# Gated linear attention layer: all values and gates ahead of the heads, parked in DRAM, instead of head by head

## The chip, the cores and the metric

The kernel runs on one core of one Trainium2 chip. The metric is the device time of one execution in microseconds (us). Three executions of the kernel before took 945.23, 946.44 and 946.85 us, median 946.44 us.

TensorE (PE in the profile) does the matrix products, with its weight loads shown apart as PEld. VectorE is DVE, ScalarE is ACT, GpSimd is POOL, and SyncE (SP) only issues DMAs here. Each engine works through its own queue of instructions strictly in the order written for it.

## The reference, cut to what matters

Two layers run on a sequence of 512 rows of 1024 channels. The first (a state-space branch and a convolution branch) is not touched by the change. The second is gated linear attention with four heads:

```python
u = rms_norm(x, norm_pre[i])
p = u @ od_w_in[j]                       # 1024 -> 2*1024 + 2*2048 + 16
q, k, v, r, lr = split(p)                # queries, keys, values, gates, low rank
g = log_sigmoid(lr @ w_gate_up + b_gate) / 16
# per head: q, k 256 wide, v 512 wide; b = running sum of g inside a chunk of 64 rows
# S_t = diag(exp(g_t)) S_{t-1} + k_t^T v_t ;  o_t = q_t S_t     (causal)
o = rms_norm(o, norm_g) * silu(r)        # per head
x = x + rms_norm(concat(o) @ od_w_out[j], norm_post[i])
```

Values and gates of a head depend only on `u` and weights. The decays `b` enter queries and keys only.

## The kernel before

**Precision and tiles.** Every product is made from operands split into a high and a low part, so one 128x128 weight tile times 512 columns costs three matmuls (high*high, high*low, low*high). Weights come in blocks of 512 KB (128 x 1024 fp32) from the list `wlist` (lines 85 to 110), in the order of use. `w_raw` (line 113) issues the load of a block on SP into one of three `wraw` buffers. `w_split` (line 134) makes the high part with a cast on ACT (line 143, two `wh` buffers) and, in this layer, the low part with a subtraction on DVE (line 149, three `wl` buffers). One block feeds 24 matmuls. `w_get` (line 167) hands out a block and has the next one split ahead.

**The second layer's stages, per head.**
- `values(h)` (line 960) and `gate(h)` (line 965): both call `proj_mv` (line 804), four weight blocks and 96 matmuls (lines 800 to 802) into four PSUM banks of the tag `mm`, one for each 128 rows. `values` splits each bank into `vh` and `vl` (line 963; `split` at line 191 is a cast on ACT, line 193, and a subtraction on DVE, line 194). `gate` puts SiLU on it (ACT, line 970) and multiplies by the norm's gain on POOL (line 971). There is one `vh` and one `vl` for all heads. Gates lie in buffers of the tag `sb`, eight in all.
- queries and keys (lines 1010 to 1064): four weight blocks, 96 matmuls by `mm_st` (line 181) with one `mm` bank a block, and then for each bank a chain on DVE, ACT and POOL that multiplies by the exponentials of the running sums of decays `bcum` and splits the result (`qr` into `qh`, `ql`; `kr` into `kh`, `kl`). `sums(h)` (line 988) is the running sum, two scans on DVE.
- scores (lines 1070 to 1093): 42 small matmuls (line 1078) into `aux` banks, three of them, masked into `at` on DVE (line 1083) and split into `ah`, `al`.
- outputs (lines 1105 to 1130): 30 matmuls (lines 1113 to 1115), in four parts of 128 rows; each part goes through a square sum on ACT, a reciprocal root of seven small DVE steps (lines 200 to 209), a product with the gate on DVE (line 1125), four transposes on PE (line 1128, one `cv` bank) and a split into `oth`, `otl`.
- the output projection: its first half (heads 0 and 1) is done at head 2 (lines 1097 to 1103) and kept in DRAM as `yp_d`; the second half comes in `proj_tail` (line 872) after head 3, whose first part again is a `proj_mv` of 96 matmuls, block by block over the channels, head 2's first.

In program order the layer is: values(0); decays (lines 976 to 996); gate(0); then for each head queries and keys, values (but for head 0), the next head's sums, scores, gate (but for head 0), at head 2 the first half of the output projection, and outputs.

**What sets the real order.** The program is planned when it is built (`TileContext(..., schedule_with_timeline_sim=True)`, line 1213): a planner plays the engines through with estimated durations, and gives each engine the ready instruction that comes first in program order. `feed()` (line 156) moves an instruction 1500 places ahead; the weight splits and `split` use it. So work that is ready fills gaps left by work that comes before it in the program. What the planner wrote is then fixed for each queue, and an instruction that is late on the chip holds all behind it on its engine.

**Temporaries.** `tmp()` (line 74) gives one of five buffers of the tag `t2`; a buffer comes free when its last reader, a DMA included, is done.

Of the kernel before, what the change touches and what calls it, by code (L numbers as in the profile page):

```python
# [9 lines left out]
F32 = mybir.dt.float32  # L10
F32R = mybir.dt.float32r
I32 = mybir.dt.int32
AF = mybir.ActivationFunctionType
ALU = mybir.AluOpType
# [3 lines left out]
P = 128  # L18
D = 1024
S = 512  # L20
KT = D // P
TT = S // P
# [9 lines left out]
HEADS = 4  # L32
# [19 lines left out]
def trunk(ctx: ExitStack, tc: tile.TileContext, A: dict, out: bass.AP, dbg: dict | None = None):  # L52
    nc = tc.nc
    V, G, SC, PE, SY = nc.vector, nc.gpsimd, nc.scalar, nc.tensor, nc.sync
# [7 lines left out]
    dram = ctx.enter_context(tc.tile_pool(name="dram", bufs=1, space=DRAM))  # L62
# [7 lines left out]
    def ps(tag="mm"):  # L70
        n = banks["bufs"][tag]
        return banks["pool"].tile([P, S], F32, tag=tag, bufs=n, name=f"ps_{tag}")

    def tmp(shape=(P, S), dt=F32, name="tmp"):
        return t2.tile(list(shape), dt, tag="t2", name=name)
# [9 lines left out]
    wlist = []  # L85
# [14 lines left out]
    for n in range(2):  # L100
        for j in range(4):
            wlist.append(A["w_out0"][n, 4 + j])
    for h in range(HEADS):
        wv, wr = ([A["w_vr"][o + h, j] for j in range(4)] for o in (0, 4))
        wqk = [A["w_qk"][2 * h + j] for j in range(2)] + [A["w_qk"][8 + 2 * h + j] for j in range(2)]
        wlist.extend(wv + wr + wqk if h == 0 else wqk + wv + wr)
        if h >= 2:
            for n in range(2):
                for j in range(4):
                    wlist.append(A["w_out1"][n, (h - 2) * 4 + j])  # L110
    wst = {"next_raw": 0, "next_split": 0, "raw": {}, "hl": {}, "low": {}}

    def w_raw():
# [42 lines left out]
    def feed():  # L156
        return tc.high_priority(offset=1500)
# [9 lines left out]
    def w_get():  # L167
        i = wcur[0]
        wcur[0] += 1
        while wst["next_split"] <= min(i + 1, len(wlist) - 1) and wst["next_split"] not in w_resident:  # L170
            w_split()
        return wst["hl"].pop(i)
# [8 lines left out]
    def mm_st(acc, w, xh, xl):  # L181
        wh, wl = w
        whv = wh.rearrange("p (k c) -> p k c", c=P)
        wlv = wl.rearrange("p (k c) -> p k c", c=P)
        for k in range(KT):
            PE.matmul(acc, whv[:, k, :], xh[:, k, :], start=(k == 0), stop=False)  # L186
            PE.matmul(acc, whv[:, k, :], xl[:, k, :], start=False, stop=False)  # L187
        for k in range(KT):
            PE.matmul(acc, wlv[:, k, :], xh[:, k, :], start=False, stop=(k == KT - 1))  # L189

    def split(h, l, src, eng=V):
        with feed():
            SC.copy(h, src)
            eng.tensor_tensor(out=l, in0=src, in1=h.bitcast(F32), op=ALU.subtract)  # L194
# [56 lines left out]
    def bigt(dt, name):  # L251
        return big.tile([P, KT, S], dt, tag="big", name=name)
# [475 lines left out]
    def sbt_(shape, dt, name):  # L728
        return sbp.tile(list(shape), dt, tag="sb", name=name)
# [30 lines left out]
    csum, vs, rstd, rt, v = ln[:, 0, :], (ln[:, 1, :], ln[:, 2, :]), ln[:, 3, :], ln[:, 4, :], ln[:, 0, :]  # L760
# [31 lines left out]
    def mm_mv(accs, w, xh, xl, k0, kt0, first, last):  # L792

        wh, wl = w
        for j in range(2):
            kt = kt0 + j
            whj, wlj = wh[:, j * S:(j + 1) * S], wl[:, j * S:(j + 1) * S]
            for tt in range(TT):
                ts_ = slice(tt * P, (tt + 1) * P)
                PE.matmul(accs[tt], xh[:, kt, ts_], whj, start=(first and j == 0), stop=False)  # L800
                PE.matmul(accs[tt], xl[:, kt, ts_], whj, start=False, stop=False)  # L801
                PE.matmul(accs[tt], xh[:, kt, ts_], wlj, start=False, stop=(last and j == 1))  # L802

    def proj_mv(xh, xl, blocks=()):
        accs = [ps("mm" if i < banks["bufs"]["mm"] else "aux") for i in range(TT)]
        for j in range(4):
            mm_mv(accs, blocks[j] if blocks else w_get(), xh, xl, 0, 2 * j, j == 0, j == 3)
        return accs

    yp = rp.tile([P, TT, D], F32, tag="r16", name="yp")  # L810
    for n in range(2):
        accs = proj_mv(yfh, yfl)
# [56 lines left out]
    u1h = bigt(F32R, "u1h")  # L869
    u1l = bigt(F32R, "u1l")  # L870
# [61 lines left out]
    L1 = ExitStack()  # L932
    LQ = ExitStack()
    pa = L1.enter_context(tc.tile_pool(name="l1a", bufs=1, side="right", reuse_waits="tile"))
    vh = pa.tile([P, TT, S], F32R, name="vh")
    vl = pa.tile([P, TT, S], F32R, name="vl")
    bcum = pa.tile([P, KT, S], F32, name="bcum")
    ng = pa.tile([P, S], F32, name="ng")
# [21 lines left out]
    def values(blocks=()):  # L960
        accs = proj_mv(u1h, u1l, blocks)
        for tt in range(TT):
            split(vh[:, tt, :], vl[:, tt, :], accs[tt])

    def gate(h):
        accs = proj_mv(u1h, u1l)
        rg = []
        for tt in range(TT):
            r_ = sbt_((P, S), F32, f"rg{h}{tt}")
            SC.activation(r_, accs[tt], AF.Silu)  # L970
            G.tensor_tensor(out=r_, in0=r_, in1=ng, op=ALU.mult)  # L971
            rg.append(r_)
        return rg

    values(vblocks)
    az = pg.tile([P, KT, S], F32, name="az")
    for kt in range(KT):
# [10 lines left out]
    def sums(h):  # L988

        for kt in (2 * h, 2 * h + 1):  # L990
            V.tensor_tensor_scan(out=bcum[:, kt, :], data0=reset, data1=bcum[:, kt, :], initial=0.0, op0=ALU.mult, op1=ALU.add)  # L991

    for kt in range(KT):
        V.tensor_sub(bcum[:, kt, :], bcum[:, kt, :], az[:, kt, :])
        if kt == 1:
            sums(0)
    rg = gate(0)
    PG.close()

    pb = L1.enter_context(tc.tile_pool(name="l1b", bufs=1, side="right", reuse_waits="tile"))  # L1000
    pq = LQ.enter_context(tc.tile_pool(name="l1q", bufs=1, side="right", reuse_waits="tile"))
    R_OFF = (0, 448, 768, 960)
    NQ = 1152
# [1 line left out]
    COL = {(0, 0): None, (0, 3): 0, (0, 2): 128, (0, 1): 256, (1, 3): 384, (1, 2): 512, (2, 3): 640}  # L1005

    yp_d = dram.tile([S, D], F32, name="yp_d")
    for h in range(HEADS):

        qh = pq.tile([P, 2, NQ], F32R, tag="qh", name=f"qh{h}")  # L1010
        ql = pq.tile([P, 2, NQ], F32R, tag="ql", name=f"ql{h}")
        kh = pq.tile([P, 2, 896], F32R, tag="kh", name=f"kh{h}")
        kl = pq.tile([P, 2, 896], F32R, tag="kl", name=f"kl{h}")
        eb, en, el = [], [], []
        for j in range(2):
            kt = 2 * h + j
# [10 lines left out]
        for j in range(2):  # L1027
# [8 lines left out]
            for i in range(4):  # L1036
                o = R_OFF[i]

                dst = qr[:, o:o + 256].rearrange("p (a t) -> p a t", t=128)[:, :, 0:64] if o + 256 <= NQ else None
                src = acc[:, i * P:(i + 1) * P].rearrange("p (a t) -> p a t", t=64)  # L1040
# [12 lines left out]
        for j in range(2):  # L1053
            acc = ps()
            mm_st(acc, w_get(), u1h, u1l)
            kr = pq.tile([P, 896], F32, tag="raw", bufs=1, name=f"kr{h}{j}")
            ec, es = el[j]
            V.tensor_mul(kr[:, 0:S], acc, en[j])
            fac = small.tile([P, 3, 2], F32, tag="fac", bufs=2, name=f"fac{h}{j}")
            V.tensor_copy(fac[:, :, 0], es[:, 0:3])  # L1060
            V.tensor_copy(fac[:, :, 1], ec.rearrange("p (i a) -> p i a", a=2)[:, 0:3, 1])
            G.tensor_tensor(out=kr[:, S:896].rearrange("p (i t) -> p i t", t=64), in0=kr[:, 0:384].rearrange("p (i t) -> p i t", t=64),  # L1062
                            in1=fac.rearrange("p i a -> p (i a)").unsqueeze(2).to_broadcast([P, 6, 64]), op=ALU.mult)
            split(kh[:, j, :], kl[:, j, :], kr)
        if h:
            values()
        if h + 1 < HEADS:
            sums(h + 1)

        ah = pb.tile([P, 1280], F32R, tag="ah", name=f"ah{h}")  # L1070
        al = pb.tile([P, 1280], F32R, tag="al", name=f"al{h}")
# [8 lines left out]
        for jj in range(4):  # L1080
# [5 lines left out]
            if jj < 3:  # L1086
                q0, n = OFFD[jj]
# [3 lines left out]
                w_ = (384, 256, 128)[jj]  # L1091
                split(ah[:, c0:c0 + w_], al[:, c0:c0 + w_], acc[:, 0:w_])
        split(ah[:, 0:S], al[:, 0:S], at.rearrange("p j t -> p (j t)"))
        if h:
            rg = gate(h)

        if h == 2:
            for n in range(2):
                accs = proj_mv(*oa)
# [3 lines left out]
                    SY.dma_start(yp_d[tt * P:(tt + 1) * P, n * S:(n + 1) * S], yt)  # L1103

        if h % 2 == 0:
            oth = pb.tile([P, KT, S], F32R, tag="oth", bufs=1, name=f"oth{h}")
            otl = bigt(F32R, f"otl{h}")
        acol = {(0, 3): 512, (0, 2): 640, (0, 1): 768, (1, 3): 896, (1, 2): 1024, (2, 3): 1152}
        for i in range(4):
# [20 lines left out]
            split(oth[:, k0:k0 + 4, i * P:(i + 1) * P], otl[:, k0:k0 + 4, i * P:(i + 1) * P], tp.rearrange("p (k t) -> p k t", t=P))  # L1130
        if h == 1:
            oa = (oth, otl)
    LQ.close()

    E1 = ExitStack()
# [9 lines left out]
    proj_tail(oth, otl, yp, bigt, x1_d, gpost1, tail1)  # L1145
    E1.close()
    L1.close()
    SBP.close()
    L0.close()

# [66 lines left out]
```

## Time and profile before

| | us |
|---|---|
| median of three executions | 946.44 |
| the profiled execution's own time | 946.38 |
| its span, first to last instruction | 944.7 |
| PE busy | 897.7 (95% of the span) |
| weight loads of PE busy | 718.9 (76%) |
| DVE busy | 641.9 (68%) |
| ACT busy | 485.1 (51%) |
| POOL busy | 245.4 (26%) |
| PE's mean granted clock | 0.981 |

Busy time is the time in which an engine works on at least one instruction. Matmuls overlap: each shows some 0.39 us from start to end, but the next starts 0.23 us later. The granted clock is the share of full speed that PE is given. A line of the timeline reads: start, duration, engine, line of the kernel, operation, result, operands, count, and in brackets the idle time before it with what ended it. The second layer's first matmuls begin shortly after 500 us.

### The profile page before, as it was taken

What the parts mean: (1) busy time and instruction counts of PE and PEld (TensorE: products, weight loads), DVE (VectorE), ACT (ScalarE), POOL (GpSimd) and SP (SyncE); (2) the same over time, 40 slices, a digit from 0 to 9 for tenths busy, and PEclk for the clock granted to TensorE, in tenths of its full rate; (3) what the DMA queues carried; (4) which work ended last, traced back from release to release, by engine and by line L of the source; (5) the groups of instructions that cost most, each with busy time, mean ns of one, the idle gap of its engine ahead of it and who ended that gap; (6) DMA issues with size and microseconds to landing.
All of it is one profiled execution on the core that took longest, in us unless ns stands there. A gap on an engine that the chain in (4) does not pass through costs nothing. (4 is left out here: it accounts for less than half of the span.)

```text
span 944.7 us, 12134 instructions
## 1 busy us (share of the span) xinstructions
PE 897.7 (95%) x4396; PEld 718.9 (76%) x4396; DVE 641.9 (68%) x1206; ACT 485.1 (51%) x693; POOL 245.4 (26%) x258
## 2 busy tenths in 40 slices
PE   5995998999999999999999979999999999999996
PEld 4873776777778877778887758888888888888875
DVE  7953999999989989832579477584483232744546
ACT  6542786786678855564444566343543242523430
POOL 2693657463123422011054002000200020000222
PEclk8998999999999999999999979999999999999998
DMA  9877987787988885288463112212212223324412
GB/s 278 228 198 194 229 199 184 178 205 204 215 220 228 210 231 179 92 224 201 153 215 124 45 63 93 84 37 82 90 67 90 73 83 135 134 89 164 193 45 89
DMA packets 54955, 142.74 MB, mean 151 GB/s; under 512 B 14256, under 2 KB 15792, under 8 KB 54896
## 3 DMA queue, kind: packets, MB, share of 16 engines
q1 hardware_dynamic: 46832, 112.62, 35.9%
q0 software_dynamic: 8064, 29.36, 17.3%
q8 instruction: 34, 0.56, 0.2%
q14 instruction: 25, 0.20, 0.1%
HBM read 95.18 MB, written 13.22 MB: 115 GB/s over the span
## 5 line engine op out<-in xcount | busy, mean ns | idle before, releaser
L143 ACT CAST wh<-wraw 128x1024 fp32r<-128x1024 f32 x126 | 132.1, 1048 | 161.4 <-PE ps_mm L801 92.5
L149 DVE TENSOR_TENSOR wl<-wraw,wh 128x1024 fp32r<-128x1024 f32 x70 | 87.0, 1243 | 115.2 <-ACT wh L143 114.8
L655 DVE SCALAR_TENSOR_TENSOR ps_cv<-h,cw,ps_cv 128x512 f32<-128x512 f32 x232 | 161.7, 745 | 2.7 <-ACT ps_cv L652 1.8
L186 PE MATMUL ps_mm<-u0h,wh 128*128 128x512 f32 x320 | 129.9, 407 | 1.0 <-ACT tmp L679 0.7
L187 PE MATMUL ps_mm<-u0l,wh 128*128 128x512 f32 x320 | 129.4, 405 | 0.0
L800 PE MATMUL ps_mm<-wh,u1h 128*128 128x512 f32 x240 | 96.2, 402 | 3.5 <-ACT wh L143 3.4
L801 PE MATMUL ps_mm<-wh,u1l 128*128 128x512 f32 x240 | 96.3, 401 | 0.8 <-DVE u1l L194 0.8
L131 POOL DMA_DIRECT2D wl<-wraw x56 | 48.9, 884 | 182.4 <-ACT wl L130 178.2
L802 PE MATMUL ps_mm<-wl,u1h 128*128 128x512 f32 x240 | 91.6, 401 | 1.6 <-DVE wl L149 1.6
L189 PE MATMUL ps_mm<-u0h,wl 128*128 128x512 f32 x320 | 82.5, 395 | 1.1 <-DMA wl<-wraw 1.1
L186 PEld LDWEIGHTS ps_mm<-u0h,wh 128*128 128x128 f32 x320 | 61.8, 193 | 16.4 <-issue 1.6
L130 ACT ACTIVATE wl<-wraw 128x1024 fp32r<-128x1024 f32 x56 | 59.2, 1057 | 25.8 <-DMA wraw<-in_w_in_dram 14.0
L187 PEld LDWEIGHTS ps_mm<-u0l,wh 128*128 128x128 f32 x320 | 61.7, 193 | 13.9 <-issue 1.1
L189 PEld LDWEIGHTS ps_mm<-u0h,wl 128*128 128x128 f32 x320 | 59.4, 188 | 14.9 <-DMA wl<-wraw 1.5
L800 PEld LDWEIGHTS ps_mm<-wh,u1h 128*128 128x128 f32 x240 | 45.9, 191 | 14.9 <-ACT wh L143 3.8
L971 POOL TENSOR_TENSOR rg<-rg,ng 128x512 f32<-128x512 f32 x16 | 24.2, 1544 | 124.6 <-ACT rg L970 124.6
L802 PEld LDWEIGHTS ps_mm<-wl,u1h 128*128 128x128 f32 x240 | 45.6, 191 | 13.1 <-DVE wl L149 2.3
L801 PEld LDWEIGHTS ps_mm<-wh,u1l 128*128 128x128 f32 x240 | 45.9, 191 | 11.7 <-DVE u1l L194 1.2
L186 PE MATMUL ps_mm<-u1h,wh 128*128 128x512 f32 x128 | 50.7, 396 | 0.0
L187 PE MATMUL ps_mm<-u1l,wh 128*128 128x512 f32 x128 | 50.5, 394 | 0.0
L1062 POOL TENSOR_TENSOR kr<-kr,fac 128x384 f32<-128x384 f32 x8 | 6.7, 837 | 124.2 <-DVE rr L205 65.1
L800 PE MATMUL ps_mm<-wh,oth 128*128 128x512 f32 x96 | 37.8, 396 | 0.5 <-ACT wh L143 0.5
(341 smaller groups left out, 1993.6 us busy)
## 6 DMA issues: line engine op xcount, KB each, us to landing
wl<-wraw POOLq DMA_DIRECT2D x56, 512.0 KB, 6.1
wraw<-in_w_in_dram SPq DMA_DIRECT2D x40, 512.0 KB, 5.2
wraw<-in_w_out_dram SPq DMA_DIRECT2D x32, 512.0 KB, 3.3
wraw<-in_w_vr_dram SPq DMA_DIRECT2D x32, 512.0 KB, 3.2
wraw<-in_w_qk_dram SPq DMA_DIRECT2D x16, 512.0 KB, 3.3
tm<-kt_d SPq DMA_DIRECT2D x8, 512.0 KB, 6.3
wraw<-in_w_glu_dram SPq DMA_DIRECT2D x8, 512.0 KB, 5.8
wraw<-in_w_pw_dram SPq DMA_DIRECT2D x8, 512.0 KB, 5.1
```

The source lines that it names most:

```text
L130: SC.activation(l, raw, AF.Copy, scale=-1.0)
L131: G.dma_start(l.bitcast(F32), raw, accum_op=ALU.add)
L143: SC.copy(h, raw)
L149: V.tensor_tensor(out=l, in0=raw, in1=h.bitcast(F32), op=ALU.subtract)
L186: PE.matmul(acc, whv[:, k, :], xh[:, k, :], start=(k == 0), stop=False)
L187: PE.matmul(acc, whv[:, k, :], xl[:, k, :], start=False, stop=False)
L189: PE.matmul(acc, wlv[:, k, :], xh[:, k, :], start=False, stop=(k == KT - 1))
L655: V.scalar_tensor_tensor(out=acc, in0=h[:, k:k + S], scalar=cw[:, c, k:k + 1], in1=acc, op0=ALU.mult, op1=ALU.add)
L800: PE.matmul(accs[tt], xh[:, kt, ts_], whj, start=(first and j == 0), stop=False)
L801: PE.matmul(accs[tt], xl[:, kt, ts_], whj, start=False, stop=False)
L802: PE.matmul(accs[tt], xh[:, kt, ts_], wlj, start=False, stop=(last and j == 1))
L971: G.tensor_tensor(out=r_, in0=r_, in1=ng, op=ALU.mult)
```

## The change

- Only gate(0) follows values(0) as before. Then all other values and gates are computed ahead of the heads: values and gates of head 1, of head 2, queries and keys of head 0, and values and gates of head 3. Weight blocks are listed in that order.
- Each value bank of heads 1 to 3 is split into two `t2` buffers and stored to DRAM (`vh_d`, `vl_d`, 256 KB each time); each gate, head 0's too, is stored to `rg_d`. All these stores are issued on SP.
- In the loop over the heads, `vh` and `vl` are loaded back (1 MB each) by DMAs that POOL issues, gates (four times 256 KB) by DMAs that SP issues.
- Queries and keys become a function; those of head h+1 stand after the scores of head h and ahead of its outputs. Each call begins with its own `sums(h)`; sums(0) no longer stands among the decays.
- The pools are nested otherwise: `oth` gets a pool of its own on the left side, scores' pool is opened after the last values.

```diff
-    for h in range(HEADS):
-        wv, wr = ([A["w_vr"][o + h, j] for j in range(4)] for o in (0, 4))
...
+    for blocks in (vr_blocks(0), vr_blocks(1), vr_blocks(2), qk_blocks(0), vr_blocks(3), qk_blocks(1), qk_blocks(2), qk_blocks(3)):
+        wlist.extend(blocks)
+    for h in range(0, HEADS, 2):
+        for n in range(2):
+            for j in range(4):
+                wlist.append(A["w_out1"][n, 2 * h + j])
...
     for kt in range(KT):
         V.tensor_sub(bcum[:, kt, :], bcum[:, kt, :], az[:, kt, :])
-        if kt == 1:
-            sums(0)
-    rg = gate(0)
     PG.close()
...
+    def keep_value(h, tt, src):
+        hi, lo = tmp(dt=F32R, name="vhi"), tmp(dt=F32R, name="vlo")
+        split(hi, lo, src)
+        SY.dma_start(vh_d[h][:, tt, :], hi.bitcast(F32))
+        SY.dma_start(vl_d[h][:, tt, :], lo.bitcast(F32))
+
+    def keep_gate(h, tt, r_, src):
+        SC.activation(r_, src, AF.Silu)
+        G.tensor_tensor(out=r_, in0=r_, in1=ng, op=ALU.mult)
+        SY.dma_start(rg_d[h][:, tt, :], r_)
+
+    def gate(h):
+        accs = proj_mv(u1h, u1l)
+        for tt in range(TT):
+            keep_gate(h, tt, sbt_((P, S), F32, f"rg{h}{tt}"), accs[tt])
+
+    def values_gate(h):
+        accs = proj_mv(u1h, u1l)
+        for tt in range(TT):
+            keep_value(h, tt, accs[tt])
+        gate(h)
+
+    gate(0)
...
-    for h in range(HEADS):
+    def queries_keys(h):
+        sums(h)
...
+        qk_of[h] = (qh, ql, kh, kl)
+
+    values_gate(1)
+    values_gate(2)
+    queries_keys(0)
+    values_gate(3)
...
+    for h in range(HEADS):
+        qh, ql, kh, kl = qk_of.pop(h)
         if h:
-            values()
-        if h + 1 < HEADS:
-            sums(h + 1)
+            G.dma_start(vh, vh_d[h])
+            G.dma_start(vl, vl_d[h])
...
-        if h:
-            rg = gate(h)
+        if h + 1 < HEADS:
+            queries_keys(h + 1)
+        rg = []
+        for tt in range(TT):
+            r_ = sbt_((P, S), F32, f"rgl{h}{tt}")
+            SY.dma_start(r_, rg_d[h][:, tt, :])
+            rg.append(r_)
```

More of the change, by code (lines that the diff above doesn't have):

```diff
@@ L102, in trunk, with vr_blocks, qk_blocks @@
             wlist.append(A["w_out0"][n, 4 + j])
-    for h in range(HEADS):
-        wv, wr = ([A["w_vr"][o + h, j] for j in range(4)] for o in (0, 4))
[L105 to L110, printed above, removed]
+    def vr_blocks(h):
+        return [A["w_vr"][o + h, j] for o in (0, 4) for j in range(4)]
+    def qk_blocks(h):
+        return [A["w_qk"][o + 2 * h + j] for o in (0, 8) for j in range(2)]
+    for blocks in (vr_blocks(0), vr_blocks(1), vr_blocks(2), qk_blocks(0), vr_blocks(3), qk_blocks(1), qk_blocks(2), qk_blocks(3)):
[4 more added lines that the diff above has]
+                wlist.append(A["w_out1"][n, 2 * h + j])
     wst = {"next_raw": 0, "next_split": 0, "raw": {}, "hl": {}, "low": {}}
@@ L963, in values @@
             split(vh[:, tt, :], vl[:, tt, :], accs[tt])
[L965 to L973, printed above, removed]
     values(vblocks)
@@ L994, in trunk @@
         V.tensor_sub(bcum[:, kt, :], bcum[:, kt, :], az[:, kt, :])
-        if kt == 1:
-            sums(0)
-    rg = gate(0)
     PG.close()
-    pb = L1.enter_context(tc.tile_pool(name="l1b", bufs=1, side="right", reuse_waits="tile"))
+    rg_d = [dram.tile([P, TT, S], F32, name=f"rg_d{h}") for h in range(HEADS)]
+    vh_d, vl_d = ([dram.tile([P, TT, S], F32, name=f"v{n}_d{h}") for h in range(HEADS)] for n in "hl")
+    def keep_value(h, tt, src):
[17 more added lines that the diff above has]
+    gate(0)
     pq = LQ.enter_context(tc.tile_pool(name="l1q", bufs=1, side="right", reuse_waits="tile"))
@@ L1007, in trunk @@
     yp_d = dram.tile([S, D], F32, name="yp_d")
-    for h in range(HEADS):
+    qk_of = {}
+    def queries_keys(h):
+        sums(h)
         qh = pq.tile([P, 2, NQ], F32R, tag="qh", name=f"qh{h}")
@@ L1064, in trunk @@
             split(kh[:, j, :], kl[:, j, :], kr)
+        qk_of[h] = (qh, ql, kh, kl)
[3 more added lines that the diff above has]
+    values_gate(3)
+    LO = ExitStack()
+    po = LO.enter_context(tc.tile_pool(name="l1o", bufs=1, side="left", reuse_waits="tile"))
+    LB = ExitStack()
+    pb = LB.enter_context(tc.tile_pool(name="l1b", bufs=1, side="right", reuse_waits="tile"))
+    for h in range(HEADS):
+        qh, ql, kh, kl = qk_of.pop(h)
         if h:
-            values()
-        if h + 1 < HEADS:
-            sums(h + 1)
+            G.dma_start(vh, vh_d[h])
+            G.dma_start(vl, vl_d[h])
         ah = pb.tile([P, 1280], F32R, tag="ah", name=f"ah{h}")
@@ L1105, in trunk @@
         if h % 2 == 0:
-            oth = pb.tile([P, KT, S], F32R, tag="oth", bufs=1, name=f"oth{h}")
+            oth = po.tile([P, KT, S], F32R, tag="oth", bufs=1, name=f"oth{h}")
             otl = bigt(F32R, f"otl{h}")
@@ L1132, in trunk @@
             oa = (oth, otl)
+    LB.close()
     LQ.close()
@@ L1147, in trunk @@
     L1.close()
+    LO.close()
     SBP.close()
```

## The prediction

> **What bounds the kernel now.** I read the page first, then busy time by stretches of the second layer, since the change touches nothing ahead of it. In the stretches the columns are the stretch, its length, busy time with counts of PE, PEld, DVE, ACT and POOL, then PE's granted clock, the DMA engines' busy share and GB/s.
>
> ```profile
> span 944.7 us, 12134 instructions
> PE 897.7 (95%) x4396; PEld 718.9 (76%) x4396; DVE 641.9 (68%) x1206; ACT 485.1 (51%) x693; POOL 245.4 (26%) x258
> ```
> ```profile
> 533.00:558.00 25.00, 19.90 (x73) 14.67 (x72) 18.00 (x23) 20.25 (x23) 0.00 (x0) 0.84 0.09 26
> 558.00:905.00 347.00, 346.48 (x1600) 284.49 (x1599) 180.12 (x407) 139.44 (x210) 32.44 (x27) 1.00 0.30 103
> 680.00:705.00 25.00, 25.00 (x119) 20.59 (x118) 21.00 (x68) 11.73 (x20) 2.38 (x3) 1.00 0.25 85
> 905.00:944.70 39.70, 31.26 (x135) 24.56 (x133) 21.04 (x51) 6.16 (x17) 10.26 (x8) 0.93 0.14 53
> ```
>
> From 558 to 905 us PE is busy for 346.48 of 347.00 us at full clock. A busy PE could still run slowly, so I looked at the pace: in the chain of waits (start, duration, what) eight matmuls of 512 columns take 1.87 us, 0.234 us each, four transposes 0.44 us and 18 score matmuls 1.99 us, 0.11 us each, and this pace holds through the stretch.
>
> ```profile
> 577.12 1.87 PE ps_mm L189 x8
> ...
> 629.25 0.44 PE ps_cv L1128 x4
> ...
> 737.47 1.99 PE ps_aux L1078 x18
> ```
>
> The change keeps every matmul. So there is nothing to win from 558 to 905 us, and what can be won lies in the stretch ahead of it, where PE stands idle for 5.1 us. The timeline of PE there:
>
> ```profile
> 547.40 0.39 PE L802 MATMUL ps_mm<-wl,u1h 128*128 128x512 f32 x1
> 551.19 0.80 PE L800 MATMUL ps_mm<-wh,u1h 128*128 128x512 f32 x1 [3.40 <-ACT wh L143]
> 551.78 0.63 PE L801 MATMUL ps_mm<-wh,u1l 128*128 128x512 f32 x1
> ...
> 556.52 2.07 PE L802 MATMUL ps_mm<-wl,u1h 128*128 128x512 f32 x4 [1.55 <-DVE wl L149]
> ...
> 560.40 0.39 PE L802 MATMUL ps_mm<-wl,u1h 128*128 128x512 f32 x1
> ```
>
> and of the two engines that it waits for:
>
> ```profile
> 546.61 1.22 DVE L991 TENSOR_TENSOR_SCAN bcum<-reset,bcum 128x512 f32<-128x512 bf16 x1
> ...
> 549.14 1.06 ACT L986 ACTIVATE az<-az 128x1024 f32<-128x1024 f32 x1
> ...
> 550.11 1.03 ACT L143 CAST wh<-wraw 128x1024 fp32r<-128x1024 f32 x1
> ...
> 551.91 3.44 DVE L991 TENSOR_TENSOR_SCAN bcum<-reset,bcum 128x512 f32<-128x512 bf16 x3
> ...
> 555.27 1.20 DVE L149 TENSOR_TENSOR wl<-wraw,wh 128x1024 fp32r<-128x1024 f32 x1
> ...
> 559.84 2.33 DVE L991 TENSOR_TENSOR_SCAN bcum<-reset,bcum 128x512 f32<-128x512 bf16 x2
> ```
>
> In gate(0), the cast of the third weight block stands on ACT behind the decays' exponentials and logarithms, and its subtraction on DVE behind three scans. After that idle time PE starts matmuls 0.43 us apart instead of 0.23. From 547.63 (the last good matmul's end of pace) to 560.40 there are 12.77 us, in which 17 matmuls run that need 17 x 0.234 = 4.0 us: the stall costs **8.8 us**, of which some 3.7 are the slow clock. This is all that the layer offers.
>
> [...]
>
> **The change, part by part.** The sum is made against the profiled execution's own 946.38 us, which is 1.7 us over its span and 0.06 below the median.
>
> *1. The early stall: 0.* Values(0), decays and gate(0) stay as they are, but for sums(0). Two scans leave their place among the decays. Yet the scans that held the subtraction at 555.27 are not these two: the layer's eight scans all run from 546.61 to 562.2 us, in the first and last row above, so those of all four heads, and later heads' scans already stood behind gate(0) in program order and were put forward into DVE's gaps. ACT's order, which costs the 3.40 us, has no scan in it. So I leave the stall. Bounds: -8.8 (it goes) to 0.
>
> *2. Values and gates in a row: +1.5.* Seven projections of 96 matmuls, 22.4 us each by 0.234, follow one another with only queries and keys of head 0 between them. Scores and outputs of other heads, which fill such joints now, all come later. The price is at the joints, since all four `mm` banks change hands there.
>
> ```profile
> L194 DVE TENSOR_TENSOR vl<-ps_mm,vh 128x512 fp32r<-128x512 f32 x16 | 11.0, 689 | 8.1 <-ACT vh L193 7.9
> L193 ACT CAST vh<-ps_mm 128x512 fp32r<-128x512 f32 x16 | 9.4, 585 | 10.8 <-PE ps_mm L802 10.1
> ```
> ```profile
> zb_d<-tmp SPq DMA_DIRECT2D x8, 256.0 KB, 4.9
> yp_d<-ypc SPq DMA_DIRECT2D x8, 256.0 KB, 2.1
> yp<-yp_d SPq DMA_DIRECT2D x1, 2048.0 KB, 8.0
> wl<-wraw POOLq DMA_DIRECT2D x56, 512.0 KB, 6.1
> ```
>
> Let the first value bank be complete at 0; three matmuls a bank, the others are at 0.7, 1.4 and 2.1 us, and the next projection reaches the fourth bank at 2.1 + 2.1 = 4.2. Today that bank is free at 2.1 + 0.59 + 0.69 = 3.4. After the change its two halves need the seventh and eighth of eight `t2` buffers where there are five. Three must have come back from their stores: they are filled by 1.3, and with 2.1 us from issue to landing back by 3.4, some 3.8 with the issues one after the other. Then the last subtraction ends at 4.5, 0.3 late. With 4.9 us (a store of that size in the first layer, where DMA is busier) it ends at 7.3, 3.1 late. Three such joints: 0.9 to 9.3 us. The DMA engines are busy for 0.30 of the time here, so I take the lower end, with 0.5 a joint: 1.5. If the planner sees the wait, PE does the other banks first and the price is nothing; so 0 to 9.3. Gates free their bank after ACT alone and cost nothing; the cover is that banks complete 0.7 us apart.
>
> *3. The loop over heads: +2.* Here PE loses its long covers. From queries and keys of head 1 to those of head 3 it has 3 x 22.4 us, and twice 30 output matmuls (7.0), 16 transposes (1.8, at 0.11) and 42 score matmuls (4.7 at 0.11): 94 us. DVE's part in these, by rows: tiles `qr`, `kr`, `otl`, `at`, `al` and `rs_t` in this order (the whole layer, columns as above, engines that do nothing left out), then groups.
>
> ```profile
> 505.00:945.00 440.00, 28.96 (x104) 9.26 (x8) 0.98 0.27 93
> 505.00:945.00 440.00, 14.22 (x16) 7.53 (x8) 6.70 (x8) 0.98 0.27 93
> 505.00:945.00 440.00, 50.70 (x128) 24.11 (x128) 10.96 (x16) 0.98 0.27 93
> 505.00:945.00 440.00, 7.57 (x20) 5.68 (x20) 2.10 (x4) 0.98 0.27 93
> 505.00:945.00 440.00, 15.69 (x40) 7.51 (x40) 7.63 (x16) 0.98 0.27 93
> 505.00:945.00 440.00, 27.93 (x116) 0.98 0.27 93
> ```
> ```profile
> L149 DVE TENSOR_TENSOR wl<-wraw,wh 128x1024 fp32r<-128x1024 f32 x56 | 69.0, 1231 | 102.8 <-ACT wh L143 102.6
> L1125 DVE SCALAR_TENSOR_TENSOR tmp<-ps_aux,rr,rg 128x512 f32<-128x512 f32 x16 | 12.0, 749 | 7.7 <-POOL rg L971 6.9
> L200 DVE TENSOR_SCALAR rs_y<-vv 128x1 int32<-128x1 int32 x23 | 3.5, 151 | 0.6
> L209 DVE TENSOR_SCALAR vv<-ss 128x1 f32<-128x1 f32 x23 | 3.4, 148 | 1.3 <-ACT junk L218 0.6 <-ACT tmp L1122 0.5
> L1033 DVE TENSOR_TENSOR es<-ec 128x4 f32<-128x4 f32 x8 | 3.3, 409 | 0.2
> L1023 DVE COPY ec<-eb 128x8 f32<-128x8 f32 x8 | 2.6, 327 | 4.0 <-ACT eb L1020 4.0
> ```
>
> A head's queries and keys: (28.96 + 14.22 + 3.3 + 2.6) / 4 = 12.3, and four weight blocks at 1.23, 4.9: 17.2 us. Outputs: 16 of 23 roots, (27.93 + 3.5 + 3.4) x 16/23 = 24.2, with 10.96 and 12.0 a quarter of 47.2: 11.8. Scores: (7.57 + 7.63 - 2.8) / 4 = 3.1 (the split of `at` stands in both rows). Together 3 x 17.2 + 2 x 14.9 = 81.4 us of DVE in 94 of PE, **86%**. The row from 680 to 705 us has 84% with PE never idle, so such a mix can be carried. But there it lasts 25 us, and here 94. If 84% is what DVE holds, PE waits 81.4/0.84 - 94 = 2.9 us; if it holds more, nothing. Late on DVE means a late subtraction of weights, with only two `wh` buffers ahead: a block is 5.6 us, cast and subtraction take 1.05 (L143) and 1.23, so some 3.3 us of slip and PE stands. I take 2.
>
> ```profile
> L143 ACT CAST wh<-wraw 128x1024 fp32r<-128x1024 f32 x56 | 58.7, 1048 | 100.7 <-PE ps_mm L801 87.7 <-PE ps_mm L187 11.8 <-issue 1.1
> ```
>
> *4. Loads of values: 0.* `vh` and `vl` can be loaded when the head before has done its last output matmul. For heads 1 and 2 queries and keys (22.4 us) lie between. For head 3 only scores (4.7) and the output projection's part on head 2's channels (48 matmuls, 11.2) can: 15.9 us. The 2 MB took 8.0 us as one load from SP; by the row of POOL's loads, which also add, four of 512 KB in turn are 24.4. So 0 to 8.5 us exposed; the plain load without the addition is the nearer row: 0. POOL's queue then holds `kr` (line 1062) behind a load that waits for outputs, but these are two heads' work apart.
>
> [...]
>
> *5. Stores, reloads, queues: 0.* 20 MB more in about 380 us is 53 GB/s beside 103 at a DMA share of 0.30. SP's stores wait behind weight loads for a free `wraw` and the reverse; three buffers are 17 us of reserve.
>
> Sum: 0 + 1.5 + 2 + 0 + 0 = +3.5, **949.9 us**.
>
> **The rivals.**
> - *All of it is hidden, 946.4.* PE had no gap through 347 us of mixed order, and the planner fills joints. Against it: the joints of values have nothing else ready, and DVE's share.
> - *The early stall goes, 941.* With the other terms 946.4 - 8.8 + 3.5; with the DVE part alone (1.55 us and the slow clock that it prolongs) some 944. For it: the scans lose their early place in the program. Against it: ACT's order has no reason to change.
> - *Head 3 stands bare, 962.* If PE's queue has outputs(3) ahead of the projection's first blocks, PE waits for `vh`: 8.5 us and 3.7 of slow clock on top of my sum. It decides when the loads take over 15.9 us, or 4.7 if the order is the bad one. Now gate(3), 22.4 us, stands there as cover.
>
> **How the numbers follow.** Some 0.2% (1.9 us) is what a measurement of this kernel tells from no change. Forecast, slower by 2 to 9 us: 0.41. Hidden: 0.27. Stall gone: 0.22. Head 3 bare: 0.10. So faster 0.22, same 0.27, slower 0.51. The likeliest case alone is 948.5 to 956; over the cases 940 to 962, which leaves out the stall gone with nothing lost and the worst of joints and head 3 together.
>
> **What would show it.** Step 1: PE's idle time before a matmul of line 800, released by the cast of line 143, near 551 us; gone, and the rival holds. Step 2: waits of PE for the low value halves at the joints, waits of ACT or DVE for stores. Step 3: DVE at 85% or more in the loop, PE waiting for line 149. Step 4: PE waiting for `vh` or `vl` after head 2's outputs. I am wrong if PE is gapless through the values, or if the time falls below 944.

## The result and the profile after

The changed kernel takes 957.12 us (median of four runs, 953.52 to 961.40), the kernel before, measured beside it, 945.84 (median of four). The ratio is **1.0123, 95% interval 1.0078 to 1.0169**: slower by some 11.6 us (11.3 between the medians), where 3.5 were forecast. The profiled execution took 957.76 us, its span is 956.0.

Busy time by stretches of the changed kernel, columns as in the prediction:

```profile
533.00:558.00 25.00, 19.48 (x76) 14.36 (x75) 17.48 (x24) 20.68 (x24) 0.00 (x0) 0.93 0.11 40
558.00:858.00 300.00, 300.00 (x1370) 245.62 (x1371) 145.87 (x321) 113.46 (x163) 34.81 (x31) 1.00 0.45 151
858.00:917.00 59.00, 50.44 (x235) 41.36 (x234) 33.46 (x89) 21.64 (x44) 1.10 (x2) 0.91 0.55 196
```

and of the kernel before in the last of them:

```profile
858.00:917.00 59.00, 58.45 (x269) 47.10 (x268) 28.31 (x56) 21.68 (x37) 9.85 (x7) 1.00 0.41 152
```

The values and gates in a row, and the heads down to the last queries and keys, run without any gap on PE, as before: 300.00 of 300.00 us. The early stall is still there. What is new lies in the last 59 us ahead of the tail, where PE is busy for 50.44 instead of 58.45 us, at a granted clock of 0.91 instead of 1.00. PE's waits over the second layer of the changed kernel (line numbers have moved: 1167 are the transposes of the outputs, 1152 to 1154 their matmuls, 804 to 806 `proj_mv`, 147 and 153 the weights' split):

```profile
PE ps_cv L1167 <- DVE vv L213: 6.9, 2, 4.3
PE ps_mm L804 <- ACT wh L147: 3.4, 1, 3.4
PE ps_mm L806 <- DVE wl L153: 2.0, 1, 2.0
PE ps_aux L1152 <- ACT ah L197: 1.7, 1, 1.7
```

These are its four longest. The second and third row are the old stall. The first and last are new; here they are on PE's timeline:

```profile
871.49 0.39 PE L806 MATMUL ps_mm<-wl,oth 128*128 128x512 f32 x1
876.20 1.11 PE L1167 MATMUL ps_cv<-ident,tmp 128*128 128x128 f32 x4 [4.32 <-DVE vv L213]
876.97 0.78 PE L1152 MATMUL ps_aux<-vh,ah 128*128 128x512 f32 x1
...
880.84 0.39 PE L1152 MATMUL ps_aux<-vh,ah 128*128 128x512 f32 x1
...
900.91 0.50 PE L1152 MATMUL ps_aux<-vh,ah 128*128 128x512 f32 x1 [1.66 <-ACT ah L197]
...
907.85 1.01 PE L1167 MATMUL ps_cv<-ident,tmp 128*128 128x128 f32 x4 [2.58 <-DVE vv L213]
908.51 0.78 PE L1152 MATMUL ps_aux<-vh,ah 128*128 128x512 f32 x1
...
911.54 0.39 PE L1153 MATMUL ps_aux<-vl,ah 128*128 128x512 f32 x1
```

Three gaps, 4.32 + 1.66 + 2.58 = 8.6 us. After the first, nine matmuls from 876.97 to 880.84 take 3.87 us in place of 9 x 0.234 = 2.1; after the last, seven from 908.51 to 911.54 take 3.03 in place of 1.6; the transposes ahead of them lose some 0.7 together. The granted clock is 0.52 in both of these stretches of matmuls and 1.00 right after each (880.84 to 885, 911.54 to 917). In all some 12.4 us, against a single gap of 0.53 us that the kernel before has at its end: that is about the whole difference of the two spans, 956.0 - 944.7 = 11.3 us.

The first gap begins when the first half of the output projection is over. ACT's timeline shows why nothing was ready then:

```profile
869.83 1.99 ACT L1141 COPY ypc<-ps_mm 128x512 f32<-128x512 f32 x3 [2.69 <-PE ps_mm L806]
871.71 1.05 ACT L147 CAST wh<-wraw 128x1024 fp32r<-128x1024 f32 x1
872.65 0.59 ACT L1141 COPY ypc<-ps_mm 128x512 f32<-128x512 f32 x1
873.13 0.61 ACT L1161 ACTIVATE tmp<-ps_aux 128x512 f32<-128x512 f32 x1
```

The last row is the square of head 2's first output part. Its three matmuls were done long before, among the projection's first; they are the first three of eighteen output matmuls that run there up to 838 us, those of three parts:

```profile
824.20 0.39 PE L1152 MATMUL ps_aux<-vh,ah 128*128 128x512 f32 x1
824.43 0.39 PE L1153 MATMUL ps_aux<-vl,ah 128*128 128x512 f32 x1
824.66 0.40 PE L1154 MATMUL ps_aux<-vh,al 128*128 128x512 f32 x1
```

The last of the three ends at 825.1, the square starts at 873.1: the part lay finished for 48 us, until the projection's last copy had been made. The kernel before has the same order (ACT again):

```profile
806.07 0.59 ACT L1102 COPY ypc<-ps_mm 128x512 f32<-128x512 f32 x1
806.55 0.61 ACT L1122 ACTIVATE tmp<-ps_aux 128x512 f32<-128x512 f32 x1
```

but there queries and keys of head 3, its values and its gate still followed, 3 x 22.4 us of matmuls to put beside the chain. The change has used them up earlier.

### The profile page after: what moved, and what is told of

Read it like the earlier page. It is cut to its first block, busy times and chain, and to the rows that moved or that the text cites. A ratio compares the mean times of both kernels' runs of the same rounds, so it can differ in the third digit from the quotient of the medians.

```text
span 956.0 us, 12285 instructions
## 1 busy us (share of the span) xinstructions
PE 902.7 (94%) x4396; PEld 723.0 (76%) x4396; DVE 640.7 (67%) x1206; ACT 481.0 (50%) x690; POOL 249.3 (26%) x264
## 5 line engine op out<-in xcount | busy, mean ns | idle before, releaser
L806 PE MATMUL ps_mm<-wl,u1h 128*128 128x512 f32 x240 | 88.3, 395 | 2.0 <-DVE wl L153 2.0
L190 PEld LDWEIGHTS ps_mm<-u0h,wh 128*128 128x128 f32 x320 | 61.6, 193 | 15.9 <-issue 1.3
L805 PE MATMUL ps_mm<-wh,otl 128*128 128x512 f32 x96 | 38.3, 399 | 0.0
```

## The experiments

Two theories stood against each other. **A, the bare chain:** at the end nothing is left to run beside the outputs' steps on ACT and DVE. **B, the reload:** head 3's values come back late. A third, C, put the loss down to the added traffic and queues in general.

**The projection at head 3.** `oth2` is a second buffer for the high outputs, from a freed one. With it the tail's low resident weights go to the first such buffer, which the excerpt does not show.

```diff
-        if h == 2:
+        if h == 3:
             for n in range(2):
                 accs = proj_mv(*oa)
...
-            oth = po.tile([P, KT, S], F32R, tag="oth", bufs=1, name=f"oth{h}")
+            oth = bigt(F32R, "oth2") if h else po.tile([P, KT, S], F32R, tag="oth", bufs=1, name="oth0")
```

> The changed kernel, with the first half of the output projection moved from head 2 (ahead of its outputs) to head 3 (ahead of its outputs); head 2's high outputs get a buffer of their own, so that they need not wait for the projection. Theory A (bare chain: in the changed kernel head 2's outputs start only when the projection is over, and PE has nothing beside their DVE and ACT steps): now scores of head 3 and 45 us of projection stand beside that chain, so the 4.3 us gap after the projection and its slow clock go: 957 becomes some 949 to 951; the gap at head 3's own outputs (2.6 us and slow clock) may stay. Theory B (the reload of head 3's values decides): the reload now has the projection as cover too, so also faster, and no gap at head 3's outputs: 946. Theory C (20 MB more of traffic and longer queues): nothing changes, 957.

Measured: 947.08 us, ratio to the kernel before 0.9998 (0.9975 to 1.0020). All three gaps are gone; PE's timeline near the end has only

```profile
904.06 0.50 PE L804 MATMUL ps_mm<-wh,oth 128*128 128x512 f32 x1 [0.35 <-ACT wh L147]
905.61 0.50 PE L806 MATMUL ps_mm<-wl,oth 128*128 128x512 f32 x1 [0.57 <-DVE wl L153]
```

This speaks against C (all stores and loads are still there), but not between A and B, and it gained more than A had expected.

**Head 3's gate back at its old place.**

```diff
-        gate(h)
+        if h < 3:
+            gate(h)
...
+        if h == 3:
+            gate(3)
         rg = []
```

> The changed kernel, but with head 3's gate back where it was before the change, after the scores of head 3 (22.4 us of PE work as cover between scores and outputs of head 3, and beside head 2's outputs). Theory A: both gaps have matmuls beside them again, all three gaps go: 945 to 948. Theory B: the reload is covered too: the same. Theory C (traffic): only one gate of 1 MB less is stored and loaded, 955 to 957.

Measured: 947.20 us, ratio 1.0004 (0.9988 to 1.0021). 22.4 us of cover at head 3 undo the loss as well. The gate is still stored and loaded back (16 stores and 16 loads of gates in this profile, as before the edit), other than the expectation has it, so this run speaks against C too.

**No reload of head 3's values.** Head 3's outputs are made with head 2's values, so this load is left out and the output is another.

```diff
-        if h:
+        if h and h < 3:
             G.dma_start(vh, vh_d[h])
             G.dma_start(vl, vl_d[h])
```

> The changed kernel without the reload of head 3's values: head 3's outputs are made with head 2's values, which leaves that load of 2 MB out and makes the result another one. Theory A (bare chain of small steps): the load was done before its use, so nothing changes: 955 to 958. Theory B (the reload decides): the gaps at head 3's outputs go, 949 to 951. Theory C: 2 of 20 MB less, 956.

Measured: 952.81 us, ratio 1.0081 (1.0053 to 1.0108), between the two theories. PE's gaps:

```profile
874.61 1.12 PE L1167 MATMUL ps_cv<-ident,tmp 128*128 128x128 f32 x4 [4.31 <-DVE vv L213]
...
904.54 0.66 PE L1167 MATMUL ps_cv<-ident,tmp 128*128 128x128 f32 x4 [2.58 <-DVE vv L213]
904.95 0.48 PE L1152 MATMUL ps_aux<-vh,ah 128*128 128x512 f32 x1
905.27 0.39 PE L1153 MATMUL ps_aux<-vl,ah 128*128 128x512 f32 x1
905.50 0.39 PE L1154 MATMUL ps_aux<-vh,al 128*128 128x512 f32 x1
```

The first and last gap stay within 0.01 us: they are A's. The middle one of 1.66 us is gone, so B has a share, but not as a late `vh`. In the changed kernel the two loads are issued at 881.76 and 882.41 us and take this long (issues, 858 to 917 us; the last column is us to landing):

```profile
vl<-vl_d POOLq DMA_DIRECT2D x1, 1024.0 KB, 6.5
vh<-vh_d POOLq DMA_DIRECT2D x1, 1024.0 KB, 8.5
```

They are there by 891, ten us before head 3's outputs begin at 900.91. But the resident weights of the tail load at the same time, and one takes twice as long as its neighbours, 6.41 us against 3.23 and 3.12 (chain of waits):

```profile
880.74 3.23 DMA wraw<-in_w_out_dram
...
886.33 6.41 DMA wraw<-in_w_out_dram
...
895.10 3.12 DMA wraw<-in_w_out_dram
```

ACT's cast of that block stands in its queue ahead of the cast of the masked scores, `ah`, whose masking on DVE had ended at 896.77:

```profile
892.76 1.05 ACT L147 CAST hres<-wraw 128x1024 fp32r<-128x1024 f32 x1 [4.09 <-DMA wraw<-in_w_out_dram]
...
898.24 1.05 ACT L147 CAST hres<-wraw 128x1024 fp32r<-128x1024 f32 x1 [3.42 <-DMA wraw<-in_w_out_dram]
...
900.25 0.62 ACT L197 CAST ah<-at 128x512 fp32r<-128x512 f32 x1
```

Without the reload the cast of that block waits 0.70 us in place of 4.09:

```profile
887.97 1.05 ACT L147 CAST hres<-wraw 128x1024 fp32r<-128x1024 f32 x1 [0.70 <-DMA wraw<-in_w_out_dram]
```

So the reload delays weights (6.41 us for one block), weights block ACT (4.09 us), and ACT holds the scores back (1.66 us of PE). The two profiled spans are 5.0 us apart. Of these 1.6 stand already ahead of the first gap (874.61 against 876.20), where the reload has not begun, 1.7 are the middle gap, and 1.7 come after the last gap, where this profile's matmuls start 0.32 and then 0.23 us apart, the changed kernel's 0.43. So in this pair of profiles the reload's own share is some 1.7 us.

**What holds head 2's outputs back.** Two things could: the five `t2` buffers, which the projection's eight copies take ahead of the squares' and products' results, and the single high output buffer `oth`, which the projection still reads. First both were mended, then each alone; the copies go to the gates' buffers, and the second buffer is made as in the first experiment.

```diff
-                    yt = tmp(name="ypc")
+                    yt = sbt_((P, S), F32, "ypc")
```

> The changed kernel, with the projection left at head 2, but its copies in other buffers than head 2's outputs use (gate buffers in place of the five temporaries), and a second buffer for the high outputs. So head 2's outputs can run under the projection. Theory A: the wait for the projection's copies was an order of buffers; the chain of head 2 and the scores of head 3 now hide under the projection, the 4.3 us gap goes with its slow clock: 948 to 951. Theory B (reload of head 3's values): the reload begins earlier, since head 2's outputs are done earlier: also faster, 946 to 949. Theory C: 957.

> The changed kernel, with the projection's copies in the gates' buffers instead of the five temporaries, and nothing else. If it is the temporaries that hold head 2's outputs back until the projection's last copies, their squares and roots now run under the projection, and of the 4.3 us gap only the transposes' split into the one high output buffer still waits: the gap shrinks to 1 to 2 us or goes. If it is the single buffer of the high outputs alone, the gap stays at 4.3 us.

> The changed kernel, with a second buffer for the high outputs, and the projection's copies left in the five temporaries. If the temporaries hold head 2's outputs back, the square of their first part still runs after the projection's last copies on ACT, and the 4.3 us gap stays. If the single buffer of the high outputs is the hold, the gap goes.

Measured: both, 949.19 us, ratio 1.0038 (1.0020 to 1.0055); the copies alone, 945.83 in a single run; the second high buffer alone, 957.77 in a single run. With the second high buffer alone ACT and PE are as in the changed kernel:

```profile
872.53 0.59 ACT L1141 COPY ypc<-ps_mm 128x512 f32<-128x512 f32 x1
873.01 0.61 ACT L1161 ACTIVATE tmp<-ps_aux 128x512 f32<-128x512 f32 x1
```
```profile
876.08 1.12 PE L1167 MATMUL ps_cv<-ident,tmp 128*128 128x128 f32 x4 [4.32 <-DVE vv L213]
```

With the copies elsewhere, ACT squares head 2's parts under the projection:

```profile
837.78 0.60 ACT L1161 ACTIVATE tmp<-ps_aux 128x512 f32<-128x512 f32 x1 [0.29 <-PE ps_aux L1154]
...
849.61 1.99 ACT L1141 COPY ypc<-ps_mm 128x512 f32<-128x512 f32 x3 [2.69 <-PE ps_mm L806]
```

It was the order in which five buffers are handed out. They were not all full in the changed kernel: the stores of the first four copies are issued by 851.2 us and take at most 2.2 us, so these buffers are free by 853.4, some 20 us ahead of the square. But the projection's last four copies come first in the order of requests.

Over more runs, this one line gives

> The kernel of e2b_ypc_only once more, now timed in pairs: the projection's copies in the gates' buffers and nothing else. The one look gave 945.8. If that buffer order is the whole of the loss, the ratio to the kernel before is 1.000 within 0.002. If the chain of head 3 still costs (as it did where the high outputs had a second buffer), 1.002 to 1.005.

947.40 us, ratio 1.0017 (1.0002 to 1.0032): all but some 1.6 us of the loss. Of PE's waits at the outputs this is left:

```profile
PE ps_cv L1167 <- DVE vv L213: 0.3, 1, 0.3
```
 Why both mends together leave gaps of 1.25 and 2.58 us that the one alone does not is not settled; it moves the tail's resident weights to other buffers too.

**The joints of the values.** Every store of a value half is issued twice.

```diff
-        SY.dma_start(vh_d[h][:, tt, :], hi.bitcast(F32))
-        SY.dma_start(vl_d[h][:, tt, :], lo.bitcast(F32))
+        for _ in range(2):
+            SY.dma_start(vh_d[h][:, tt, :], hi.bitcast(F32))
+            SY.dma_start(vl_d[h][:, tt, :], lo.bitcast(F32))
```

> The changed kernel with every store of a value half issued twice (6 MB more, and each temporary buffer held for two stores). By the prediction's working of the joints (five buffers, 0.3 us late with stores of 2.1 us each) the buffers come back some 2 to 3 us later and each of three joints costs 2 to 3 us, a gap of PE that its timeline shows between 590 and 715 us: 960 to 966. If the planner puts other banks' matmuls into the wait, or the joint has more room than was worked out, no gap shows and the time is 953 to 961.

Measured in a single run: 963.50 us. Among values and gates there is one gap:

```profile
644.70 0.50 PE L804 MATMUL ps_mm<-wh,u1h 128*128 128x512 f32 x1 [0.91 <-DVE vlo L198]
```

So the joint I had worked out exists, but even twice the stores cost PE only 0.9 us at one of three, not 2 to 3 at each. The time lies in the first range, but not for the reason given there. The rest of the 6 us over the changed kernel's median is not from there: PE's wait for `u1l` at the beginning of the second layer stands at 523.19 us in this profile and at 519.63 in the changed kernel's, 3.6 us later, and nothing ahead of it was edited; the waits at the end are longer too, 2.19 us for `ah` in place of 1.66. The single run does not tell more.

**The early stall.** gate(0)'s four blocks are split into buffers of their own, ahead of the decays; once in the changed kernel, once in the kernel before, and together with the late projection and with the moved copies. The excerpt shows the edit of the kernel before.

```diff
+    gw = GW.enter_context(tc.tile_pool(name="gw", bufs=1, side="right", reuse_waits="tile"))
+    gblocks = [w_get_into((gw.tile([P, 1024], F32R, name=f"gwh{j}"), gw.tile([P, 1024], F32R, name=f"gwl{j}"))) for j in range(4)]
     az = pg.tile([P, KT, S], F32, name="az")
...
-    rg = gate(0)
+    rg = gate(0, gblocks)
```

> The changed kernel, with the four weight blocks of gate(0) split into buffers of their own ahead of the decays (so their casts stand before the exponentials on ACT). If the early stall is what the prediction says, the order of ACT and DVE behind a cast that has only two buffers, then the waits of 3.4 and 2 us near 552 us and the slow clock after them go, and the time is 7 to 9 us under the changed kernel, some 948 to 950. If PE waits there for something else (the weights' arrival, say), it stays at 957.

> The kernel before, with the same four blocks of gate(0) split ahead of the decays. By the same reading 8 to 9 us under the kernel before: 937 to 939. If the stall has another cause, 946.

> Both repairs of the changed kernel: the projection's first half at head 3, and gate(0)'s blocks split ahead of the decays. If the two losses are apart from each other, 947 less 8 to 9: 938 to 940, under both kernels, and level with the kernel before that has the early split alone, since parking values and gates then costs and brings nothing. If values and gates ahead of the heads bring something that the end had hidden, it falls below that one by more than 2 us.

With the moved copies ("the same" is the changed kernel with that one line):

> The same with gate(0)'s weight blocks split ahead of the decays. If the early stall and the bare chain at the end are apart from each other, 6 to 8 us below the kernel before: ratio 0.992 to 0.994, level with the kernel before that has the early split alone. Below 0.992: values and gates ahead of the heads bring something of their own.

| kernel | us | ratio to the kernel before |
|---|---|---|
| changed, early split | 949.81 | 1.0039 (1.0024 to 1.0054) |
| before, early split | 940.08 | 0.9938 (0.9915 to 0.9961) |
| changed, late projection, early split | 940.01 | 0.9940 (0.9924 to 0.9955) |
| changed, moved copies, early split | 940.31 | 0.9945 (0.9923 to 0.9967) |

The stall of 3.4 us is gone in all four, and the reading of it holds. By the ratios its worth is 5.9 us in the kernel before (3.7 to 8.0) and some 7.9 in the changed one; 8.8 lies above the first interval and is not excluded by the second. A smaller wait comes up ahead of it, in all four 1.5 to 2.0 us, here in the kernel before with the early split, where the low-rank factors now come late:

```profile
535.31 0.96 PE L982 MATMUL ps_mm<-lrs,gws 96*128 96x512 f32 x3 [1.54 <-DVE lrs L959]
```

All but the first beat both kernels. That the two mended versions of the changed kernel land level with the kernel before, all three with the early split, says what values and gates ahead of the heads bring by themselves: nothing that shows beyond these intervals, some 0.2% to either side.

## Why the prediction was right or wrong

The direction and the range held; 957.1 lies inside 940 to 962. The sum of 3.5 us did not: each of its two terms is zero, and the loss came from a place that had a zero in the sum. So that the time lies in the range is luck: its upper end was the time of a rival whose mechanism did not come about. By its own sign, PE gapless through the values, the prediction is wrong.

1. *Early stall, 0:* right. It stands in the changed kernel's PE waits with 3.4 and 2.0 us, and the scans' place did not matter. As its price 8.8 was probably somewhat high: mended, it gives 5.9 us in the kernel before, some 7.9 in the changed one.
2. *Values in a row, +1.5:* it measured 0. The wait for buffers is real: in the changed kernel ACT and DVE wait three times, 2.7 us together, for stores of the high halves. But PE shows no gap there, 300.00 of 300.00 us, though the stores took longer than the 2.1 us that I had used (issues; the last column is us to landing). That the planner puts other banks' matmuls into the wait is argued, not shown.

```profile
vh_d<-vhi SPq DMA_DIRECT2D x12, 256.0 KB, 2.8
vl_d<-vlo SPq DMA_DIRECT2D x12, 256.0 KB, 3.1
```

3. *Loop over heads, +2:* it measured 0 too. From the first matmul of head 1's queries to the last split of head 3's keys:

```profile
729.00:833.00 104.00, 104.00 (x511) 87.12 (x511) 77.23 (x223) 49.03 (x81) 13.33 (x16) 1.00 0.49 157
```

DVE works 77.23 us where I had 81.4, in 104 us of PE where I had 94: the planner mixed 34 matmuls of the output projection into it (8 us). So DVE stands at 74%, not 86%, less than the 84% that the kernel before carries for 25 us, and PE has no gap. The stretch also stopped too early: I ended it at head 3's queries and keys, and did not ask what stands beside the chain of outputs(2) once the projection is over.
4. *Loads of values, 0:* this is the step that failed, by its question. I compared the cover of 15.9 us with one transfer, and the transfer indeed landed in time, 9.1 us from the first issue to the last landing. But the cover itself was not free to run: the output projection's part on head 2's channels needs head 2's outputs, and these waited for the `t2` buffers behind the projection's copies. When it did run, it was spent before head 3's outputs began: its 48 matmuls stand between 881.5 and 899 us, so the chain of head 3's first parts had nothing beside it either. That the square comes behind the copies was to be seen in the trace of before, where it follows the last copy at once. What is 0 in the sum measured some 11 us, of which the reload's traffic has some 1.7 (the middle gap) and the bare chains the rest. To the reader of the trace the question is not only how long the cover is, but whether it waits for the same thing as what it should cover.
5. *Traffic, 0:* right for the stores. Not quite for the reload, which made one weight block 6.41 us long in the one place where ACT had no reserve.

The rival "head 3 bare", 962, named the place, the lost cover of gate(3) and the slow clock, and was nearest in size. Its mechanism, PE waiting for `vh`, is not what the runs show, and its price of slow clock was too high: the matmuls after the two new stalls lose 1.8 and 1.4 us, not 3.7. "All of it is hidden" would have been right but for one order of buffers: with the copies moved the ratio is 1.0017.

## What to carry to other kernels

When work is moved to the front, ask what is left at the end for the last dependent chain to run beside; a gapless engine says only that its fillers suffice where they stand now. A chain that is late in the trace of before and hidden there is the first to show when its cover moves, so look for results that lie finished (here 48 us) and for the buffer that holds them. Before moving 134 us of matmuls (six projections of 22.4 us) for their order, try the instructions that cause the only stall: here four weight blocks split ahead gave 5.9 us, and the large reordering, mended, gave nothing.

## What the runs showed of the hardware

A gap of 2.58 us was followed by seven matmuls 0.43 us apart in the changed kernel; without the reload the same gap was followed by matmuls 0.32 and then 0.23 us apart (the lines of both stand above). After the gap of 3.38 us near 552 us the changed kernel starts its first matmuls 0.34 and 0.26 us apart, and those after them 0.43:

```profile
552.50 0.50 PE L804 MATMUL ps_mm<-wh,u1h 128*128 128x512 f32 x1 [3.38 <-ACT wh L147]
552.84 0.46 PE L805 MATMUL ps_mm<-wh,u1l 128*128 128x512 f32 x1
553.10 0.63 PE L804 MATMUL ps_mm<-wh,u1h 128*128 128x512 f32 x1
553.52 0.63 PE L805 MATMUL ps_mm<-wh,u1l 128*128 128x512 f32 x1
```

So whether a gap of some 3 us costs its length or half as much again (the matmuls after the 2.58 us lost 1.4 us in one profile and 0.1 in the other), and when the slow pace sets in, differs from gap to gap. What decides it is not shown by any run here, nor whether it is a part of why runs of one kernel spread over several us (26 runs of the kernel before beside the first experiments: 943.50 to 950.96).
